# Early products parked in DRAM, value weights split once, gathers tied to single mixing jobs, and four buffers for the sine products

## The chip, the cores and the metric

The kernel runs on one core of one Trainium2 chip. The metric is the device time of one execution in microseconds; the median of the runs counts. PE is the matrix engine, PEld its weight loads, DVE the vector engine, ACT the scalar engine, POOL the GpSimd engine, and SP the engine that issues most loads.

## The reference

One layer of an encoder on 1024 tokens of width 1024, all in fp32. Cut to what matters:

```python
h = _swiglu(_rms_norm(x, g1a), w1_in, w1_out)          # 1024 -> 2 x 2816 -> 1024
x = x + 0.5 * _rms_norm(h, g1b)
m = _token_mixing(_rms_norm(x, gma), w_mix_in, ...)
x = x + _rms_norm(m, gmb)
h = _swiglu(_rms_norm(x, g2a), w2_in, w2_out)
x = x + 0.5 * _rms_norm(h, g2b)

def _token_mixing(u, ...):
    rq, rk, rv, rg, nq, nk, nv, g_ret, g_na = split(u @ w_in)
    q, k = rotary(rq), rotary(rk) * 128**-0.5            # 4 heads of 128
    y = bidirectional retention(q, k, rv)                # 4 heads of 256
    y_ret = (silu(rg) * headnorm(y)) @ w_ret_out
    y_na = neighbourhood_attention(nq, nk, nv) @ w_na_out   # 8 heads of 64, on a 16 x 64 token grid
    return (sigmoid(g_ret) * y_ret + sigmoid(g_na) * y_na) @ w_out
```

## The kernel before

**Precision.** Each fp32 operand is split into a high part (a cast on ACT, line 62) and a low part (a subtraction on DVE, line 63); three matmuls, lines 94 to 96, then make one product of 128 x 128 by 128 x 512: high times high, low times high, high times low. A split weight half is called a piece. Its parts are the tiles `wh` and `wl`, eight buffers each; the raw weights lie in `wraw`, four buffers of 128 x 1024.

**Pairs.** The wide projections run as Strassen-Winograd products on two weight blocks at a time. One such job (`Pairs.run`) makes seven products of 12 matmuls each with the factors `a11`, `s2`, `a12`, `s3`, `s1`, `a22`, `s4` of the activations, and DVE forms the sums of weights (lines 552, 553, 565, 571 or 582) and adds the results (556 to 587). The first feed-forward layer is 22 jobs, the mixing stage 14.

**The start.** `first_factors` normalizes x, transposes its first half, and forms the factors. `a11` and `a12` come from the first half of the tokens and are there first; `s2`, `s3`, `s1`, `a22` and `s4` need the second half and much of DVE. Meanwhile `Pairs.lead` gives PE the two products of a job that need `a11` and `a12` alone, 24 matmuls a job: for jobs 3, 4 and 5 (results copied to SBUF), 0, 1 and 2 (left in PSUM), and 6 (in the two other PSUM banks). A job begun in this way has 60 matmuls left of 84. Between these leads the steps of `first_factors` are written into the program.

**The mixing stage.** Jobs 0 to 3 are queries and keys of the neighbourhood attention, 4, 6, 8 and 10 those of the retention, which `rotate` turns by cosine and sine; 5, 7, 9 and 11 are its gates, 12 and 13 others. Jobs 3, 12 and 13 have been begun earlier and their early products lie in DRAM (`far`, loaded at lines 548 and 549). `rotate` multiplies by the sine into a tile `t` (line 1089), by the cosine in place (1090), stores this, and then has `t` added to the store by two DMAs from POOL (1094, 1095). `t` comes from the same ring of six buffers (`ev`) as the four results of a job. A rotary job also splits the first half of the next job's weights ahead. After job 3 the values of the second half of the tokens are projected (`vproj`), and four DRAM-to-DRAM copies on SP (`nvg<-nv`, line 1443) gather them by column block for the neighbourhood attention.

**The values of the retention.** During the neighbourhood attention (`na_cores`) PE gets other matmuls as filler: first `vproj` for the two column halves of `wrv`. It goes over the tokens in three groups and for each group loads four blocks of weights and splits eight pieces, so 24 loads and 48 pieces in all.

**Order.** A scheduler sets a fixed order of instructions on each engine from dependencies, priorities and its own estimates; `c.after` adds an order between two instructions for it, without a wait on the chip. On ACT, DVE and POOL, and in the queue of SP, an instruction that waits holds up those behind it.

Of the kernel before, what the change touches and what calls it, by code (L numbers as in the profile page):

```python
# [11 lines left out]
F32 = mybir.dt.float32  # L12
# [7 lines left out]
P = 128  # L20
D = 1024
S = 1024
KT = D // P
# [5 lines left out]
NHP = 4  # L29
# [6 lines left out]
KEY_OFF = (0, 8, 24, 32)  # L36
# [399 lines left out]
class Pairs:  # L436
# [49 lines left out]
                    self.begun[i][j] = far[i][j]  # L486
        self.far = far

    def lead(self, save=None, between=(), on_pool=(), abreast=1, extra=0, early=False):

        def split(i):
            if i not in self.fetched:
                self.fetch(i)
            w = self.fetched[i]
            self.ready[i] = self.c.piece(w[:, :512])
            self.fetched[i] = [None, self.c.piece(w[:, 512:])]

        n = self.held + self.saved
        tiles = [i for i in (*range(self.held, n), *range(self.held), *range(n, n + extra)) if i not in self.begun]
        while tiles:  # L500
            group, tiles, abreast = tiles[:abreast], tiles[abreast:], 1
            for i in group:
                if i not in self.fetched:
                    self.fetch(i)
            g = [self.fetched.pop(i) for i in group]
            eng = self.c.nc.gpsimd if group[0] in on_pool else None
            tag = ("ps", 6) if group[0] < n else ("pt", 2)
            ps = [self.products("a11", [self.ready.pop(i) if i in self.ready else w[:, :512] for i, w in zip(group, g)],
                                eng, tag),
                  self.products("a12", [w[1] if isinstance(w, list) else w[:, 512:] for w in g], eng, tag)]  # L510
            if early and tiles:
                split(tiles[0])
            if between:
                f = between.pop(0)()
                if f is not None:
                    between.append(f)
            for i, *pair in zip(group, *ps):
                if self.held <= i < n:
                    sb = [save(), save()]
                    for a, b in zip(sb, pair):  # L520
                        self.c.nc.scalar.copy(a, b)
                    pair = sb
                    self.kept.add(i)
                self.begun[i] = pair

    def behind(self, e):
# [729 lines left out]
def trunk_layer(ctx: ExitStack, tc, x, xt, g1a, w1i, w1o, g1b, gma, wmt, wnv, wrv, logits, dtab, rope, bias,  # L1256
                wro, wno, wmo, gmb, g2a, w2i, w2o, g2b, out):
    nc = tc.nc
# [5 lines left out]
    c = Core(tc, const, wpool, psum, dram)  # L1264
# [3 lines left out]
    def dt(name, shape):  # L1268
        return dram.tile(shape, F32, name=name)
# [8 lines left out]
        "dec": dt("dec", [P, 536]), "far": dt("far", [3, 2, P, 512]), "sr": dt("sr", [8, P, S]), "sn": dt("sn", [8, P, S]), "z": dt("z", [8, P, S]), "m": dt("m", [8, 2, P, S]),  # L1278
    }

    def rows(a):
# [12 lines left out]
    with tc.tile_pool(name="fin1", bufs=1, reuse_waits="tile") as fp:  # L1294
        def lead():
            return early.tile([P, 512], F32, tag="lead", name="lead", bufs=6)

        def sums():
            return early.tile([P, 4, P], F32, tag="cmb", name="cmb", bufs=4).rearrange("p k t -> p (k t)")

        halves = [[sums() for _ in range(2)] for _ in range(2)] + [[lead() for _ in range(2)] for _ in range(2)]
        fin = Pairs(c, wx, [(w1i[i], w1i[FT + i]) for i in LeftFactors.order], 3, 3)
        steps = first_factors(c, wx, fp, g0, halves, sums, lead, pad, x, xt, g1a,
                              lambda j: fin.fetch(3 + j, nc.gpsimd if j < 2 else None))
        next(steps)
        fin.lead(lead, [lambda: next(steps)] * 4, (3, 4), 2, 1)
        for _ in steps:
            pass
        tail = ffn_in(c, fin, fp, LeftFactors(c, early, fp, gl[0]), 40)
# [13 lines left out]
    ahead = {}  # L1323
# [9 lines left out]
    def xh(t, k):  # L1333

        return a21 if (t, k) == (1, 0) else wx.op(("a11", "a12", None, "a22")[2 * t + k])
# [2 lines left out]

    def vproj(src, groups, done):

        for toks in groups:
            banks = {t: c.bank() for t in toks}
            for k in range(KT):
                if k % 2 == 0:
                    w = ahead.pop(k // 2) if k // 2 in ahead else c.load_w(src[k // 2])
                    if k > 3 and qk:
                        c.after(c.fetch, qk)
                        qk.clear()
                for t in toks:
                    tt = slice((t % 4) * P, (t % 4 + 1) * P)  # L1350
                    c.mm3(banks[t], [q[:, k % 4, tt] for q in xh(t // 4, k // 4)], w[k % 2], k == 0, k == KT - 1)
                    yield
            for t in toks:
                done(t, banks[t])
# [43 lines left out]
    with tc.tile_pool(name="pa", bufs=1, reuse_waits="tile") as pa:  # L1398
# [4 lines left out]
        def half():  # L1403
            return pa.tile([P, 512], F32, tag="ev", name="ev", bufs=6)
# [6 lines left out]
        for i, (_, _, f, g, fn) in enumerate(jobs):  # L1411
            parts = {}

            def part(j):
                parts[j] = half()
                return parts[j]

            def done(j):
                h = j % 2
                dst = (f, g)[j // 2][:, h * 512:(h + 1) * 512]  # L1420
                while swaps:
                    swaps.pop()()
                if fn == "rotary":
                    swaps.append(rotate(c, half(), parts[j], *tabs[h], dst, [] if j == 0 else [mx.ahead]))
                    return
                if fn is not None:
                    nc.scalar.activation(parts[j], parts[j], fn)
                c.store(dst, parts[j])
            mx.run(i, part, done, fn == "rotary")
            if i == 2:  # L1430
                x1pool = pool(x1_stack, "x1b", "right")
                a21[:] = [x1pool.tile([P, 4, 512], F32R, name=f"a21{q}") for q in "hl"]
                for k in range(2):
                    raw = c.raw(d["a21"][:, 2 * k:2 * k + 2].rearrange("p k t -> p (k t)"))
# [12 lines left out]
    m_stack, o_stack = ExitStack(), ExitStack()  # L1447
# [237 lines left out]
```

## Time and profile before

| what | before |
|---|---|
| median of three runs | 2220.22 us (2219.85 to 2223.01) |
| profiled execution, its own time | 2219.05 us |
| its span | 2217.2 us |
| granted clock of PE, mean | 0.998 |
| PE busy | 2189.7 us, 99% |
| PEld busy | 1825.6 us, 82% |
| DVE busy | 1589.4 us, 72% |
| ACT busy | 973.8 us, 44% |
| POOL busy | 582.7 us, 26% |
| DMA moved | 448.30 MB |

A busy PE is the union of modelled matmul times, and one matmul of 512 columns is shown with about 390 ns although a new one starts every 0.22 to 0.23 us. So the count of matmuls in a stretch tells more of PE than its busy time does: 90 in 20 us is the most that stretches of 512-column matmuls show. The first feed-forward layer lies at 0 to 652 us, the mixing stage's jobs at about 710 to 985, the neighbourhood attention at 985 to 1152, retention and output projections up to 1525, the second feed-forward layer after that.

### The profile page before, as it was taken

To read this page: it belongs to the slowest core of one execution; us is meant where nothing else is said; L and a number is where in the kernel's file an instruction comes from. 1 tells how busy PE (TensorE), PEld (TensorE's weight loads), DVE (VectorE), ACT (ScalarE), POOL (GpSimd) and SP (SyncE) were. 2 spreads that over 40 slices of the span, in tenths; PEclk is the share of its full clock that TensorE was granted. 3 is DMA by queue.
4 is the path that set the end of the run, shared out by engine and by line. 5 is a ranking of instruction groups with operands and counts; after the bars stand their busy time and mean duration, and the time that the engine had idled before them with its cause. 6 is when DMAs were issued, how large, how long until landed. Compare 5 with 4: busy or idle time off the path is not lost.

```text
span 2217.2 us, 29770 instructions
## 1 busy us (share of the span) xinstructions
PE 2189.7 (99%) x10232; PEld 1825.6 (82%) x10232; DVE 1589.4 (72%) x2796; ACT 973.8 (44%) x1999; POOL 582.7 (26%) x760
## 2 busy tenths in 40 slices
PE   8999999999999999999999999999999999999998
PEld 6788888888888887888888888888888888888887
DVE  8998878665569756779876677553899787867444
ACT  6444434332345322268875565322544343433232
POOL 1121212168422122311101222101112121216942
PEclk9999999999999999999999999999999999999999
DMA  5454434598656564577764466785436343549865
GB/s 218 142 205 148 169 126 179 203 382 298 232 183 200 192 183 133 144 228 237 227 202 144 149 201 225 260 307 190 167 142 221 135 176 133 180 165 372 279 223 185
DMA packets 151734, 448.30 MB, mean 202 GB/s; under 512 B 19488, under 2 KB 46240, under 8 KB 149472
## 3 DMA queue, kind: packets, MB, share of 16 engines
q1 hardware_dynamic: 108592, 308.22, 41.2%
q0 software_dynamic: 42992, 138.20, 17.3%
q8 instruction: 81, 1.33, 0.2%
q14 instruction: 69, 0.57, 0.1%
HBM read 299.78 MB, written 150.75 MB: 203 GB/s over the span
## 4 chain that ended last, share of the span: by engine, by line
PE 89%; DVE 7%; issue 2%; DMA 1%; POOL 1%; ACT 1%; POOLq 0%; SPq 0%; DVEq 0%; ACTq 0%
PE ps L95 27%; PE ps L94 27%; PE ps L96 27%; PE pt L95 1%; PE pt L94 1%; PE pt L96 1%; DVE wl L63 1%; PE ps L962 1%; PE pt L981 1%; POOL rstd L104 0%; PE pt L133 0%; DMA gt<-in_dram 0%; PE pt L1195 0%; DMA vl<-rv 0%; DMA g0s<-gth 0%
## 5 line engine op out<-in xcount | busy, mean ns | idle before, releaser
L63 DVE TENSOR_TENSOR wl<-wraw,wh 128x512 fp32r<-128x512 f32 x472 | 315.1, 688 | 54.6 <-ACT wh L62 54.2
L62 ACT CAST wh<-wraw 128x512 fp32r<-128x512 f32 x476 | 273.5, 618 | 142.8 <-PE ps L95 67.0
L94 PE MATMUL ps<-wh,g 128*128 128x512 f32 x548 | 214.1, 391 | 0.4 <-DVE tmp L231 0.4
L95 PE MATMUL ps<-wl,g 128*128 128x512 f32 x548 | 213.6, 390 | 0.0
L96 PE MATMUL ps<-wh,g 128*128 128x512 f32 x548 | 213.3, 389 | 0.0
L63 DVE TENSOR_TENSOR wl<-w,wh 128x512 fp32r<-128x512 f32 x77 | 79.8, 1057 | 83.1 <-ACT wh L62 82.9
L63 DVE TENSOR_TENSOR wl<-x,wh 128x512 fp32r<-128x512 f32 x77 | 79.5, 1049 | 77.2 <-ACT wh L62 75.6
L62 ACT CAST wh<-t 128x512 fp32r<-128x512 f32 x58 | 36.1, 622 | 210.7 <-DVE t L553 206.7
L94 PEld LDWEIGHTS ps<-wh,g 128*128 128x128 f32 x548 | 102.9, 188 | 21.9 <-DVE tmp L231 0.7
L95 PEld LDWEIGHTS ps<-wl,g 128*128 128x128 f32 x548 | 102.9, 188 | 21.3 <-DVE wl L63 0.5
L96 PEld LDWEIGHTS ps<-wh,g 128*128 128x128 f32 x548 | 102.8, 188 | 21.4
L94 PE MATMUL ps<-a11h,wh 128*128 128x512 f32 x276 | 108.7, 395 | 1.5 <-ACT a11h L62 1.5
L94 PE MATMUL ps<-a22h,wh 128*128 128x512 f32 x280 | 109.9, 393 | 0.0
L95 PE MATMUL ps<-a22l,wh 128*128 128x512 f32 x280 | 109.3, 390 | 0.0
L96 PE MATMUL ps<-a22h,wl 128*128 128x512 f32 x280 | 109.0, 389 | 0.0
L95 PE MATMUL ps<-a11l,wh 128*128 128x512 f32 x276 | 107.9, 391 | 1.0 <-DVE a11l L63 0.8
L94 PE MATMUL ps<-a12h,wh 128*128 128x512 f32 x276 | 108.2, 393 | 0.0
L96 PE MATMUL ps<-a11h,wl 128*128 128x512 f32 x276 | 107.7, 390 | 0.5 <-DVE wl L63 0.5
L96 PE MATMUL ps<-a12h,wl 128*128 128x512 f32 x276 | 107.5, 390 | 0.0
L95 PE MATMUL ps<-a12l,wh 128*128 128x512 f32 x276 | 107.5, 389 | 0.0
L568 DVE TENSOR_TENSOR c<-ps,gt 128x512 f32<-128x512 f32 x44 | 30.4, 691 | 91.5 <-PE ps L96 91.3
L69 POOL DMA_DIRECT2D g0a<-gth x33 | 17.9, 547 | 296.4 <-ACT gth L651 272.3
(439 smaller groups left out, 6316.1 us busy)
## 6 DMA issues: line engine op xcount, KB each, us to landing
wraw<-in_dram SPq DMA_DIRECT2D x203, 512.0 KB, 4.5
g<-g0s SPq DMA_DIRECT2D x44, 512.0 KB, 4.6
g<-g1s SPq DMA_DIRECT2D x44, 512.0 KB, 4.5
g<-g0a SPq DMA_DIRECT2D x33, 512.0 KB, 4.4
g<-g1a SPq DMA_DIRECT2D x33, 512.0 KB, 4.5
g0s<-gth POOLq DMA_DIRECT2D x44, 256.0 KB, 3.9
g0s<-cmb POOLq DMA_DIRECT2D x44, 256.0 KB, 3.8
g1s<-gth POOLq DMA_DIRECT2D x44, 256.0 KB, 3.9
```

The source lines that it names most:

```text
L62: self.done = [nc.scalar.copy(h, src).ins, (eng or nc.vector).tensor_tensor(l, src, hf, ALU.subtract).ins]
L63: (eng or nc.vector).tensor_tensor(l, src, hf, ALU.subtract).ins]
L69: self.nc.gpsimd.dma_start(dst, src)
L94: mm(ps, a[0], b[0], start=start, stop=False, skip_group_check=again)
L95: mm(ps, a[0], b[1], start=False, stop=False, skip_group_check=again)
L96: self.tail = mm(ps, a[1], b[0], start=False, stop=stop, skip_group_check=again).ins.name
L568: self.last = tt(c21, p7, c12, ALU.add).ins
L962: nc.tensor.matmul(bv, q[:, rg * P:(rg + 1) * P], k, start=n == 0, stop=n == 1)
L981: nc.tensor.transpose(pt[:, j * P:(j + 1) * P], s[:, i % 2, (i // 2) * P:(i // 2 + 1) * P], c.ident)
```

## The change

Four edits.

1. `lead` gets jobs 8, 11 and 14 as well, between jobs 5 and 0 of its list. Their two products are copied from PSUM to the tiles `t2` (two buffers) and stored to DRAM (`far1`). In `run` they are loaded back as the far jobs of the mixing stage are. `far2` is allocated and not used.
2. `vproj` keeps the eight pieces of a column half for its three groups of tokens.
3. The four gathers are written one behind each of the mixing jobs 5 to 8, ordered after the job's last addition.
4. The sine products `t` get a ring of four buffers of their own (`evt`).

```diff
-    def lead(self, save=None, between=(), on_pool=(), abreast=1, extra=0, early=False):
+    def lead(self, save=None, between=(), on_pool=(), abreast=1, extra=0, early=False, far={}):
...
         n = self.held + self.saved
-        tiles = [i for i in (*range(self.held, n), *range(self.held), *range(n, n + extra)) if i not in self.begun]
+        self.far = far
+        tiles = [i for i in (*range(self.held, n), *far, *range(self.held), *range(n, n + extra)) if i not in self.begun]
...
-            tag = ("ps", 6) if group[0] < n else ("pt", 2)
+            tag = ("ps", 6) if group[0] < n or group[0] in far else ("pt", 2)
...
+                if i in far:
+                    for a, b in zip(far[i], pair):
+                        e = self.c.wpool.tile([P, 512], F32, tag="t2", name="t2", bufs=2)
+                        self.c.nc.scalar.copy(e, b)
+                        self.c.store(a, e)
+                    pair = far[i]
                 self.begun[i] = pair
...
-        fin.lead(lead, [lambda: next(steps)] * 4, (3, 4), 2, 1)
+        fin.lead(lead, [lambda: next(steps)] * 4, (3, 4), 2, 1,
+                 far={i: d["far1"][n] for n, i in enumerate((8, 11, 14))})
...
     def vproj(src, groups, done):
 
+        w = []
         for toks in groups:
             banks = {t: c.bank() for t in toks}
             for k in range(KT):
-                if k % 2 == 0:
-                    w = ahead.pop(k // 2) if k // 2 in ahead else c.load_w(src[k // 2])
+                if k == len(w):
+                    w += ahead.pop(k // 2) if k // 2 in ahead else c.load_w(src[k // 2])
...
-                    c.mm3(banks[t], [q[:, k % 4, tt] for q in xh(t // 4, k // 4)], w[k % 2], k == 0, k == KT - 1)
+                    c.mm3(banks[t], [q[:, k % 4, tt] for q in xh(t // 4, k // 4)], w[k], k == 0, k == KT - 1)
...
-                    swaps.append(rotate(c, half(), parts[j], *tabs[h], dst, [] if j == 0 else [mx.ahead]))
+                    swaps.append(rotate(c, pa.tile([P, 512], F32, tag="evt", name="evt", bufs=4), parts[j], *tabs[h], dst, [] if j == 0 else [mx.ahead]))
...
-                for cb in range(4):
-                    nc.sync.dma_start(d["nvg"][cb].rearrange("t (r c) d -> (t r) c d", r=4),
-                                      d["nv"][:, KEY_OFF[cb]:KEY_OFF[cb] + 32, :])
+            if NHP < i <= NHP + 4:
+                cb = i - NHP - 1
+                c.after(nc.sync.dma_start(d["nvg"][cb].rearrange("t (r c) d -> (t r) c d", r=4),
+                                          d["nv"][:, KEY_OFF[cb]:KEY_OFF[cb] + 32, :]).ins, [mx.end.name])
```

**DVE at the start.** The last step of the factors `s2` and `s3` and what follows; `wl<-wraw` are the low parts of the leads' pieces, line 420 the sums for `s1`, line 552 the first sum of job 0. Before:

```order
L63 TENSOR_TENSOR s2l<-cmb,s2h 128x512
L63 TENSOR_TENSOR wl<-wraw,wh 128x512 x2
L552 TENSOR_TENSOR wraw<-wraw 128x512
L420 TENSOR_TENSOR g<-g,gt 128x512
L553 TENSOR_TENSOR t_616<-wraw 128x512
```

Now, at the same place:

```order
L63 TENSOR_TENSOR s2l<-cmb,s2h 128x512
L63 TENSOR_TENSOR wl<-wraw,wh 128x512 x6
L420 TENSOR_TENSOR g<-g,gt 128x512
L63 TENSOR_TENSOR wl<-wraw,wh 128x512 x2
L63 TENSOR_TENSOR s1l<-g,s1h 128x512
```

The pieces of jobs 8, 11 and 14 have taken the places of jobs 0, 1 and 2 between the earlier steps, and those of 0, 1, 2 and 6 stand here. From here to the low part of job 0's third product stand 30 instructions before and 34 now.

**DVE in the mixing stage.** The end of job 6 before (`wraw_7320` is the first weight block of job 7, `wraw_7213` the second one of job 6; lines 1089 and 1090 are `rotate`):

```order
L584 TENSOR_TENSOR ev_7296<-ps_7335,ev_7296 128x512
L63 TENSOR_TENSOR wl_7323<-wraw_7320,wh_7322 128x512
L1089 TENSOR_TENSOR ev_7331<-ev_7326,tab_6228 128x512
L1089 TENSOR_TENSOR ev_7351<-ev_7296,tab_6228 128x512
L1090 TENSOR_TENSOR ev_7326<-ev_7326,tab_6227 128x512
L1090 TENSOR_TENSOR ev_7296<-ev_7296,tab_6227 128x512
L63 TENSOR_TENSOR wl_7357<-wraw_7213,wh_7356 128x512
L552 TENSOR_TENSOR wraw_7320<-wraw_7379,wraw_7320 128x512
L553 TENSOR_TENSOR t2_7381<-wraw_7379,wraw_7320 128x512
```

Now the end of job 7 (line 591 was 584 and adds the product with `a22`, line 594 was 587 and adds the last one, with `s4`; `wraw_7557` is the first weight block of job 8):

```order
L584 TENSOR_TENSOR ev_7510<-ps_7493,ev_7491 128x512
L586 TENSOR_TENSOR ev_7429<-ps_7493,ev_7429 128x512
L591 TENSOR_TENSOR ev_7491<-ps_7516,ev_7491 128x512
L594 TENSOR_TENSOR ev_7429<-ps_7536,ev_7429 128x512
L63 TENSOR_TENSOR wl_7564<-wraw_7557,wh_7563 128x512
L559 TENSOR_TENSOR wraw_7557<-wraw_7559,wraw_7557 128x512
L560 TENSOR_TENSOR t2_7561<-wraw_7559,wraw_7557 128x512
```

Before, a low part that job 6 itself still needs (`wl_7357`) stood behind four instructions of `rotate`. Now jobs 4 to 7 have their splits spread between their additions, and job 8's first split stands behind job 7's last addition.

**SP in the mixing stage.** Before, around the gathers (7211 and 7213 are the weights of job 6, 7320 and 7379 those of job 7):

```order
L73 DMA wraw_7211<-in_7_dram 128x1024
L73 DMA wraw_7213<-in_7_dram 128x1024
L1443 DMA nvg_97<-nv_96 16x16384 x4
L73 DMA wraw_7320<-in_7_dram 128x1024
L73 DMA wraw_7379<-in_7_dram 128x1024
```

Now (7352 and 7412 are the weights of job 7, 7557 and 7559 those of job 8, 7872 is one of job 10):

```order
L73 DMA wraw_7352<-in_7_dram 128x1024
L73 DMA wraw_7412<-in_7_dram 128x1024
L1453 DMA nvg_97<-nv_96 16x16384 x3
L73 DMA wraw_7557<-in_7_dram 128x1024
L73 DMA wraw_7559<-in_7_dram 128x1024
...
L73 DMA wraw_7872<-in_7_dram 128x1024
L1453 DMA nvg_97<-nv_96 16x16384
```

The gathers have moved behind two more weight loads, three of them still in a row, and the fourth behind six more.

More of the change, by code (lines that the diff above doesn't have):

```diff
@@ L1277, in trunk_layer @@
         "rv": dt("rv", [TT, P, D]), "rg": dt("rg", [8, P, S]), "ry": dt("ry", [8, P, S]),
-        "dec": dt("dec", [P, 536]), "far": dt("far", [3, 2, P, 512]), "sr": dt("sr", [8, P, S]), "sn": dt("sn", [8, P, S]), "z": dt("z", [8, P, S]), "m": dt("m", [8, 2, P, S]),
+        "dec": dt("dec", [P, 536]), "far": dt("far", [3, 2, P, 512]), "far1": dt("far1", [3, 2, P, 512]), "far2": dt("far2", [3, 2, P, 512]), "sr": dt("sr", [8, P, S]), "sn": dt("sn", [8, P, S]), "z": dt("z", [8, P, S]), "m": dt("m", [8, 2, P, S]),
     }
```

## Prediction

> **What bounds the kernel now.** I read the page's head first, then the stretches of 20 us, then what PE waits for.
>
> ```profile
> span 2217.2 us, 29770 instructions
> PE 2189.7 (99%) x10232; PEld 1825.6 (82%) x10232; DVE 1589.4 (72%) x2796; ACT 973.8 (44%) x1999; POOL 582.7 (26%) x760
> ```
>
> PE is busy for all but 27.5 us, and the change takes no matmul away. So it can only win what PE loses in gaps, and everything hangs on where these lie. The stretches (columns: length, then busy us and instructions of PE, PEld, DVE, ACT, POOL, granted clock, DMA share, GB/s):
>
> ```profile
> 0.00:20.00 20.00, 11.99 (x56) 9.20 (x57) 11.56 (x18) 12.36 (x25) 7.66 (x12) 1.00 0.91 349
> 40.00:60.00 20.00, 19.43 (x86) 15.77 (x85) 19.81 (x34) 10.17 (x16) 0.00 (x0) 1.00 0.24 80
> 60.00:80.00 20.00, 16.95 (x62) 12.96 (x62) 16.23 (x27) 7.56 (x13) 0.75 (x1) 0.83 0.31 95
> 100.00:120.00 20.00, 19.44 (x85) 15.24 (x84) 19.78 (x34) 9.05 (x17) 1.82 (x4) 1.00 0.40 142
> 120.00:140.00 20.00, 19.19 (x84) 15.05 (x83) 18.83 (x32) 8.59 (x16) 7.50 (x14) 1.00 0.63 235
> 720.00:740.00 20.00, 19.23 (x85) 15.63 (x84) 15.75 (x29) 6.50 (x10) 2.70 (x5) 1.00 0.39 136
> 800.00:820.00 20.00, 20.00 (x90) 16.57 (x89) 13.14 (x22) 2.77 (x5) 3.59 (x6) 1.00 0.66 201
> 840.00:860.00 20.00, 17.48 (x76) 13.81 (x76) 15.41 (x25) 3.05 (x6) 7.46 (x10) 1.00 0.47 104
> 940.00:960.00 20.00, 20.00 (x90) 16.57 (x89) 14.96 (x25) 10.62 (x16) 3.52 (x6) 1.00 0.73 200
> 980.00:1000.00 20.00, 19.56 (x100) 16.51 (x99) 15.98 (x44) 16.26 (x38) 2.15 (x3) 1.00 0.59 196
> 1000.00:1020.00 20.00, 19.48 (x117) 16.92 (x117) 18.12 (x52) 15.84 (x45) 2.19 (x3) 1.00 0.88 259
> 2200.00:2220.00 20.00, 9.58 (x43) 7.60 (x41) 10.51 (x15) 2.17 (x6) 5.43 (x6) 0.86 0.28 105
> ```
>
> Full rate is 90 matmuls of 512 columns in 20 us, 0.222 us each (row 800 to 820). Against 90, PE lacks 4 matmuls in 40 to 60, 28 in 60 to 80, 5 and 6 in 100 to 140, 5 in 720 to 740 and 14 in 840 to 860. At 0.222 us that is 0.9, 6.2, 1.1, 1.3, 1.1 and 3.1 us. The first and the last row are the kernel's start and end, which the change does not touch. In the rows at 980 and 1000 forms are mixed, and the idle 0.44 and 0.52 us count. All within reach is thus 9.5 us in the first feed-forward layer, 4.2 in the mixing stage and 1.0 in the attention.
>
> **The long early loss.** In the order of time, with what ended the idle time in brackets:
>
> ```profile
> 60.73 0.39 PE L95 MATMUL ps<-s1l,wh 128*128 128x512 f32 x1
> 63.40 0.69 DVE L63 TENSOR_TENSOR wl<-wraw,wh 128x512 fp32r<-128x512 f32 x1
> 64.14 0.79 PE L96 MATMUL ps<-s1h,wl 128*128 128x512 f32 x1 [3.02 <-DVE wl L63]
> 64.73 0.63 PE L94 MATMUL ps<-s1h,wh 128*128 128x512 f32 x1
> 69.65 0.70 PE L94 MATMUL ps<-s4h,wh 128*128 128x512 f32 x1
> 70.19 0.39 PE L95 MATMUL ps<-s4l,wh 128*128 128x512 f32 x1
> ```
>
> PE stands with job 0's third product until DVE has made that piece's low part, and DVE (19.81 of 20 us busy in the stretch before) was still making factors. The next 13 matmuls, 64.14 to 70.19, take 6.05 us where 13 x 0.222 = 2.9 would do: the granted clock is down (0.83 over the stretch). So a wait of about 3.2 us cost 3.1 more.
>
> **Part 1, early products of jobs 8, 11 and 14.** PE gets 3 x 24 = 72 matmuls, 72 x 0.222 = 16.0 us, ahead of job 0, and has them less in jobs 8, 11 and 14. DVE gets 4 instructions more ahead of the awaited split (34 for 30). Their price and that of ACT's casts:
>
> ```profile
> L63 DVE TENSOR_TENSOR wl<-wraw,wh 128x512 fp32r<-128x512 f32 x472 | 315.1, 688 | 54.6 <-ACT wh L62 54.2
> L62 ACT CAST wh<-wraw 128x512 fp32r<-128x512 f32 x476 | 273.5, 618 | 142.8 <-PE ps L95 67.0
> ```
>
> 315.1 / 472 = 0.67 us, so the split comes 4 x 0.67 = 2.7 us later while PE comes 16.0 later. Of the 3.2 us it lacked, 16.0 - 2.7 - 3.2 = 10.1 us become slack: the stall goes whole, and with it the slow clock (-6.2), and the 0.9 of 40 to 60, where PE waits for a copy on ACT that stands behind a factor:
>
> ```profile
> PE ps L94 <- ACT gt L551: 0.6, 1, 0.6
> ```
>
> On ACT come 6 casts and 6 copies at 0.62, 7.4 us, into stretches where it is idle (9.83 of 20 us at 40 to 60); the leads that PE does first cover them. If that cover fails, the next thing late is the high part of a lead's piece.
>
> The two later losses look alike:
>
> ```profile
> 102.91 0.50 PE L94 MATMUL ps<-s2h,wh 128*128 128x512 f32 x1 [0.56 <-ACT wh L62]
> 131.57 0.50 PE L94 MATMUL ps<-s2h,wh 128*128 128x512 f32 x1 [0.81 <-ACT wh L62]
> ```
>
> They are 28.66 us apart, the time of two begun jobs; 120 matmuls need 26.7. DVE (19.78 busy in the row 100 to 120) sets that pace. Slack won earlier isn't carried on whole, since DVE must wait for PE's results between; but the new order has its splits of jobs 0 and 1 ahead of those results, one or two instructions (0.67 to 1.3 us) in front of where they were, and each of the losses is 1.1 to 1.3. Bounds: none and all of 2.4; I take 1.8, as the first should vanish and the second halve. In jobs 8, 11 and 14 DVE has as much per job as in other begun jobs, but full jobs of 84 matmuls (18.7 us) stand around each, where the loss does not occur: 0.
>
> The parked results cost 6 stores of 256 KB and 6 loads, and three weight blocks are fetched a second time. The mixing stage does the same with its far jobs:
>
> ```profile
> far<-ev POOLq DMA_DIRECT2D x6, 256.0 KB, 5.6
> ev<-far SPq DMA_DIRECT2D x6, 256.0 KB, 4.4
> SPq L548 <- DMA rq<-ev: 6.3, 1, 6.3
> ```
>
> There SP once stood 6.3 us for a buffer with weight loads queued behind it, and PE still ran at 90 (row 940 to 960). I take 0. The added addition per far job (c11 is loaded, not read from PSUM) is 0.67 us on DVE, hidden by the longer neighbours.
>
> **Part 2, kept value splits.** 16 loads, 32 casts and 32 subtractions go: 19.8 us of ACT and 21.4 of DVE, all beside PE work. In that stage PE waits for splits twice, and only the second lies in the second group of tokens:
>
> ```profile
> 1008.11 0.50 PE L95 MATMUL ps<-wl,a11h 128*128 128x512 f32 x1 [0.52 <-DVE wl L63]
> ```
>
> -0.5. All eight buffers stay held until the third group; the second half's first piece then has the rest of that group to be made, 7 x 6 matmuls, 9.3 us, against 1.3 for cast and subtraction, so no wait.
>
> **Parts 3 and 4, gathers and sine buffers.** The gathers landed in 10.1 us and PE was full (row 800 to 820); DVE lost 4.1 us waiting for a sine buffer, in the same full row. By themselves both are worth 0:
>
> ```profile
> nvg<-nv SPq DMA_DIRECT2D x4, 10.1
> 813.90 0.69 DVE L1089 TENSOR_TENSOR ev<-ev,tab 128x512 f32<-128x512 f32 x1 [1.36 <-DMA rq<-ev]
> 818.52 0.69 DVE L1089 TENSOR_TENSOR ev<-ev,tab 128x512 f32<-128x512 f32 x1 [2.72 <-DMA rq<-ev]
> ```
>
> What counts is the order of DVE that comes with them. The loss at 840 to 860:
>
> ```profile
> 847.99 0.39 PE L96 MATMUL ps<-a22h,wl 128*128 128x512 f32 x1
> 848.41 0.69 DVE L584 TENSOR_TENSOR ev<-ps,ev 128x512 f32<-128x512 f32 x1 [1.43 <-PE ps L96]
> 849.02 0.68 DVE L63 TENSOR_TENSOR wl<-wraw,wh 128x512 fp32r<-128x512 f32 x1
> 849.62 1.29 DVE L1089 TENSOR_TENSOR ev<-ev,tab 128x512 f32<-128x512 f32 x2
> 849.76 0.50 PE L96 MATMUL ps<-a11h,wl 128*128 128x512 f32 x1 [0.48 <-DVE wl L63]
> 852.02 0.69 DVE L63 TENSOR_TENSOR wl<-wraw,wh 128x512 fp32r<-128x512 f32 x1
> 852.77 0.51 PE L96 MATMUL ps<-s4h,wl 128*128 128x512 f32 x1 [2.04 <-DVE wl L63]
> ```
>
> DVE makes the low part behind four rotary instructions while PE stands. In the new order this place is regular: -3.1. But job 8's first split now stands behind job 7's last addition. The rows price that: from the start of the product's last matmul (847.99) to the first matmul with the new low part (849.76) are 1.77 us, and three matmuls cover 0.67: +1.1. The clock stays, as it did after 2.04 us here. Net -2.0; bounds -3.1 and, if the old loss comes back whole in job 8, 0. The wait at 720 to 740 has the same order before and now: 0.
>
> **The sum.** -6.2 - 0.9 - 1.8 - 0.5 - 2.0 = -11.4 us. The profiled execution took 2219.05 (its span and 1.85 around it) and so becomes 2207.7; the median of the runs shown, 2220.22, stands 1.2 higher, so I forecast 2208.8.
>
> **The clock, by rows and by a page.** The rows say: 3.2 us of waiting was followed by half rate for 6.05. The Trainium skill, "TensorE: Matmul & The Clock Gate", Part 1, says that PE falls to half its clock after an idle window of about 3.4 us, a window that runs freely, and is let up again after about 3.4 us of work. Half the rate agrees; here less waiting sufficed and the half rate lasted longer. By the page the slow stretch would be worth 1.7 us and not 3.1, and the sum -10.0; I go by the rows.
>
> **Rivals.**
> - *DVE keeps the pace.* The two later losses stay (+1.8) and job 8 gets the whole old loss (+2.0): -7.6, about 2212.6. For it: DVE is 95 to 99% busy there. Against it: in the new order the splits stand earlier.
> - *The early part gives little.* If `t2`'s two buffers hold up ACT until stores land, a lead's cast behind them comes late, and PE stands among the leads instead. A lead takes 24 x 0.222 = 5.3 us and a store 5.6 in the far row above, so 0.3 per lead is likely at worst, 1 us in all; only if POOL's stores took twice as long would 3 x 5.3 = 16 be lost against 8.9. A third of that, 5 us, gives 2213.8, and with no change in the mixing stage 2215.8: within 0.2% of no change (4.4 us, about what a measurement of this kernel can tell).
> - *SP blocks the far jobs; slower.* The load of a far result waits for a buffer of job 5, 8 or 11 whose stores are on POOL, and the weights of the job after it queue behind. If SP stood longer there than the weights are ahead, about one job or 18.7 us, PE would stand in three jobs. With 3.2 + 3.1 us each (wait and slow clock, as at 64) that is 18.9 - 11.4 = +7.5, 2227.7; it decides from 3 us of waiting per job on. Against it stands the 6.3 us row above without loss.
> - *The gathers aren't one per job.* The order shows three in a row still, so that edit does not do what it says; its effect is in the order of DVE alone, and is in the sum.
>
> **How the numbers follow.** As forecast within 3 us: 0.62. DVE keeps the pace: 0.24. Little from the early part: 0.10, of which most stays within 0.2% or just past it. Blocked far jobs or another new wait: 0.04. The low end has all losses gone: 9.5 + 3.1 + 0.5 = 13.1, 2207.1, less a microsecond for the spread of runs: 2206. The high end takes in the first rival and part of the second: 2214. Faster by over 0.2% 0.88, within 0.2% 0.08, slower 0.04.
>
> **What would show it.** Right: no row under 88 matmuls between 40 and 140 us and a granted clock of 1.00 there; PE at 90 in the stretch where it now has 76, and one wait for `wl` of about 1 us some 20 us later, at job 8's start; one wait for `wl` fewer in the attention; about 32 fewer casts and subtractions. Wrong: a clock below 1.00 anywhere past 20 us, PE waits for casts among the leads, or for far results at jobs 8, 11 and 14.

## The result and the profile after

| | before | after |
|---|---|---|
| median of 21 runs each | 2220.22 us (2218.36 to 2223.56) | 2217.51 us (2215.02 to 2220.59) |
| profiled execution | 2219.05 us | 2220.59 us |

The ratio is 0.9984, 95% interval 0.9978 to 0.9991: 2.7 us faster by the medians and 2.0 to 4.9 us by the interval, where 11.4 were forecast and 2206 to 2214 was the range. The execution that was profiled after the change is the slowest of its 21, so its trace is read for places and for what waits; what an edit is worth is taken from the comparisons. Its head:

```profile
span 2218.8 us, 29691 instructions
PE 2192.1 (99%) x10232; PEld 1828.2 (82%) x10232; DVE 1572.3 (71%) x2767; ACT 960.7 (43%) x1970; POOL 588.3 (27%) x766
```

DVE has 29 instructions less, ACT 29 less. The stretches that answer to those of before (length, then busy us and instructions of PE, PEld, DVE, ACT, POOL, granted clock, DMA share, GB/s):

```profile
60.00:80.00 20.00, 20.00 (x90) 16.33 (x88) 15.91 (x27) 10.56 (x18) 0.00 (x0) 1.00 0.15 52
100.00:120.00 20.00, 19.79 (x86) 15.57 (x85) 19.20 (x33) 8.69 (x15) 7.51 (x14) 1.00 0.63 237
120.00:140.00 20.00, 19.71 (x87) 15.98 (x86) 18.28 (x31) 7.58 (x14) 6.45 (x12) 1.00 0.62 224
140.00:160.00 20.00, 18.82 (x81) 15.08 (x82) 19.79 (x34) 10.98 (x20) 2.35 (x5) 1.00 0.42 144
700.00:720.00 20.00, 16.57 (x71) 13.41 (x70) 9.36 (x27) 4.86 (x8) 1.10 (x2) 0.95 0.42 139
720.00:740.00 20.00, 20.00 (x79) 16.30 (x78) 18.55 (x47) 6.31 (x12) 2.28 (x5) 0.87 0.40 132
840.00:860.00 20.00, 20.00 (x90) 16.54 (x89) 15.48 (x25) 4.55 (x8) 9.18 (x12) 1.00 0.52 124
860.00:880.00 20.00, 18.00 (x72) 14.14 (x71) 11.50 (x18) 6.84 (x12) 2.26 (x4) 0.91 0.33 96
1000.00:1020.00 20.00, 20.00 (x118) 17.49 (x119) 14.52 (x48) 13.82 (x40) 1.10 (x2) 1.00 0.63 178
```

Three of them before:

```profile
140.00:160.00 20.00, 20.00 (x90) 16.57 (x89) 19.06 (x33) 8.46 (x15) 6.40 (x12) 1.00 0.70 247
700.00:720.00 20.00, 20.00 (x90) 16.53 (x89) 18.56 (x58) 9.76 (x19) 1.82 (x3) 1.00 0.56 199
860.00:880.00 20.00, 20.00 (x90) 16.57 (x89) 13.63 (x22) 8.16 (x15) 3.94 (x6) 1.00 0.62 185
```

The long early loss is gone (62 matmuls before, 90 now, clock 1.00), and so is the one at 840 to 860. Three new ones stand in their place: 9 matmuls at 140 to 160, 19 and 11 at 700 to 740, 18 at 860 to 880, the last two with a lower clock. A matmul that reaches over the edge of a row is counted in both rows, so the balance is taken from counts that run from the kernel's start: PE is 31 matmuls ahead of before at 80 us, 36 at 140, 30 at 200 and at 700, 5 at 740, 19 at 860 and 1 at 880. At full rate one starts every 0.227 us (857.71 to 860.66 in the trace after: 13 of them), so 30 are 6.8 us. The early gain is there, and nearly all of it is lost again at 700 to 740 and at 860 to 880.

**At 719: a load of 4 KB behind weights.** From the timeline after, by engine: SP's queue, DVE, PE (numbers: start, duration; in brackets the idle time ahead and what ended it):

```profile
691.29 14.29 SPq L73 DMA_DIRECT2D wraw<-in_dram  x3
705.63 2.08 SPq L1418 DMA_DIRECT2D tab<-in_dram  x4
707.75 0.91 SPq L1057 DMA_DIRECT2D decx<-in_dram  x1
...
716.64 0.18 DVE L1060 TENSOR_SCALAR dect<-decx 128x8 f32<-128x8 f32 x1 [9.67 <-DMA decx<-in_dram]
718.26 0.69 DVE L571 TENSOR_TENSOR ev<-ps,ev 128x512 f32<-128x512 f32 x1
...
719.00 0.79 PE L94 MATMUL ps<-s1h,wh 128*128 128x512 f32 x1 [3.43 <-DVE ev L571]
725.10 0.40 PE L96 MATMUL ps<-a22h,wl 128*128 128x512 f32 x1
```

The same load and its first use before:

```profile
701.08 0.48 SPq L1050 DMA_DIRECT2D decx<-in_dram  x1
...
712.21 0.19 DVE L1053 TENSOR_SCALAR dect<-decx 128x8 f32<-128x8 f32 x1
...
722.23 0.68 DVE L564 TENSOR_TENSOR ev<-ps,ev 128x512 f32<-128x512 f32 x1
```

After job 3's products DVE computes the decays of the retention from the small table `decx`. Before, SP issued that load 11.1 us ahead of its use. Now a pair of weight loads, which wait for their buffers, stands ahead of the tables in SP's queue: the program comes to this place 6.6 us earlier (the transposes ahead of the mixing stage begin at 622.4 us instead of 629.0), `decx` is issued 6.7 us later, and it lands 8.9 us after its issue instead of 5.8. DVE stands 9.67 us, line 571 behind it, and PE behind line 571. DVE's order has changed too: the addition of line 571 (564 before) stood behind the whole computation of the decays, whose last instruction starts at 721.88, and now stands behind the first eight instructions that follow from `decx`. From 719.00 to 725.10 there are 14 matmuls, 0.44 us each.

**At 871: a cast behind four activations.** The timeline after, at the start of job 8:

```profile
869.02 0.69 DVE L594 TENSOR_TENSOR ev<-ps,ev 128x512 f32<-128x512 f32 x1 [2.03 <-PE ps L96]
...
869.79 0.63 ACT L1436 ACTIVATE ev<-ev 128x512 f32<-128x512 f32 x1 [2.13 <-DVE ev L594]
870.33 0.60 ACT L62 CAST wh<-wraw 128x512 fp32r<-128x512 f32 x1
...
870.98 0.50 PE L94 MATMUL ps<-a11h,wh 128*128 128x512 f32 x1 [2.00 <-ACT wh L62]
875.23 0.39 PE L95 MATMUL ps<-a11l,wh 128*128 128x512 f32 x1
```

ACT makes the high part of job 8's first piece only after the last silu of job 7, which waits for job 7's last addition. The two loads of its raw weights were issued at 855.1 and 855.7 and landed within 4.7 to 6.1 us, so these are not what is late. Ten matmuls then take 4.25 us, 0.43 each.

**At 141: a buffer that is still being stored.** The factors of the first layer are split into `gth` (high part, four buffers) and stored from POOL:

```profile
134.98 0.62 ACT L658 CAST gth<-cmb 128x512 fp32r<-128x512 f32 x1 [4.26 <-DMA g0a<-gth]
135.63 0.69 DVE L659 TENSOR_TENSOR cmb<-cmb,gth 128x512 fp32r<-128x512 f32 x1 [0.63 <-ACT gth L658]
137.33 0.69 DVE L659 TENSOR_TENSOR cmb<-cmb,gth 128x512 fp32r<-128x512 f32 x1 [1.01 <-ACT gth L658]
137.94 0.69 DVE L559 TENSOR_TENSOR wraw<-wraw 128x512 f32<-128x512 f32 x1
141.19 0.50 PE L94 MATMUL ps<-s2h,wh 128*128 128x512 f32 x1 [1.47 <-ACT wh L62]
```

A cast waits for a store to land, DVE waits for the cast, and the sums of the next job's weights (line 559) stand behind. DVE was busy for most of the stretch, but it was also waiting, twice.

### The profile page after: what moved, and what is told of

Same layout as the page of the kernel before. It is cut to its first block, busy times and chain, and to the rows that moved or that the text cites. A ratio compares the mean times of both kernels' runs of the same rounds, so it can differ in the third digit from the quotient of the medians.

```text
span 2218.8 us, 29691 instructions
## 1 busy us (share of the span) xinstructions
PE 2192.1 (99%) x10232; PEld 1828.2 (82%) x10232; DVE 1572.3 (71%) x2767; ACT 960.7 (43%) x1970; POOL 588.3 (27%) x766
## 4 chain that ended last, share of the span: by engine, by line
PE 90%; DVE 3%; issue 2%; DMA 2%; ACT 2%; POOL 1%; SPq 0%; POOLq 0%; DVEq 0%; ACTq 0%
PE ps L95 28%; PE ps L94 28%; PE ps L96 28%; PE pt L95 1%; PE pt L96 1%; PE pt L94 1%; PE pt L988 1%; PE ps L969 1%; DMA g0s<-gth 1%; PE pt L133 0%; POOL rstd L104 0%; DMA vl<-rv 0%; DMA decx<-in_dram 0%; DVE wl L63 0%; ACT wh L62 0%
## 5 line engine op out<-in xcount | busy, mean ns | idle before, releaser
L63 DVE TENSOR_TENSOR wl<-wraw,wh 128x512 fp32r<-128x512 f32 x440 | 292.7, 686 | 59.1 <-ACT wh L62 58.4
L62 ACT CAST wh<-wraw 128x512 fp32r<-128x512 f32 x444 | 255.9, 618 | 149.8 <-PE ps L95 65.7
L94 PE MATMUL ps<-s1h,wh 128*128 128x512 f32 x232 | 91.5, 394 | 3.4 <-DVE ev L571 3.4
L62 ACT CAST wh<-w 128x512 fp32r<-128x512 f32 x77 | 46.6, 620 | 110.9 <-PE pt L96 54.5
```

The lines of the kernel that those rows point to most:

```text
L62: self.done = [nc.scalar.copy(h, src).ins, (eng or nc.vector).tensor_tensor(l, src, hf, ALU.subtract).ins]
L63: (eng or nc.vector).tensor_tensor(l, src, hf, ALU.subtract).ins]
L94: mm(ps, a[0], b[0], start=start, stop=False, skip_group_check=again)
```

## The experiments

Each of the first three losses got a kernel that takes its supposed cause away from the changed kernel, or undoes the edit. All ratios are to the kernel before. After that come the edits one at a time, and the versions with several causes removed. A difference to the changed kernel, in us, is one of medians that were taken at different times. By the ratios and their intervals it is 4.4 us, give or take 3.1, without edit 4, and 2.0, give or take 2.5, for the fifth buffer; so the smaller differences rest on the rows, and the time alone does not show them.

### Without edit 4

```diff
-swaps.append(rotate(c, pa.tile([P, 512], F32, tag="evt", name="evt", bufs=4), parts[j], ...
+swaps.append(rotate(c, half(), parts[j], ...
```

> The changed kernel without edit 4: the sine products come from the ring of six again; the other three edits stay. The changed kernel lost 26 matmuls (30 for 4 before) at 700 to 740, where PE stood 3.43 us for line 571 on DVE, and DVE had stood 9.67 us for the load decx of the decays; SP had issued that load behind a pair of weight loads that waited for their buffers. Theory A: edit 4 alone moves the table and decay loads behind that pair. Then the stall goes and this kernel takes 2217.5 - 5.6 = about 2212 us, with decx issued some 20 us before DVE needs it and a clock of 1.00 at 700 to 740. Rival B: the early products of edit 1 bring the mixing stage to this place 7 us earlier and the loads are late whatever their order: then the stall stays, about 2217.5. The loss of 18 matmuls at 860 to 880 stays by both.

Measured: 2212.06 us, ratio 0.9964 (0.9952 to 0.9977). From its timeline (SP) and then its stretches:

```profile
693.75 0.48 SPq L1057 DMA_DIRECT2D decx<-in_dram  x1
```

```profile
700.00:720.00 20.00, 19.22 (x85) 15.61 (x84) 17.80 (x60) 7.07 (x14) 1.24 (x3) 1.00 0.25 86
720.00:740.00 20.00, 20.00 (x90) 16.57 (x89) 16.80 (x27) 6.57 (x11) 4.18 (x8) 1.00 0.57 198
860.00:880.00 20.00, 18.00 (x78) 14.11 (x77) 14.99 (x24) 7.52 (x14) 1.63 (x3) 1.00 0.40 145
```

`decx` is issued 14.0 us earlier than with edit 4 and the stall is gone: PE waits 0.78 us for line 571, as it did before, and the time is that of theory A. `decx` is issued 11.2 us ahead of its use, not the 20 that were expected. The clock stays 1.00 at job 8's start too, so not all of the difference to the changed kernel need come from 719. Four more buffers in a pool, meant for DVE's rotary work 100 us later, moved other loads in SP's queue. Why the scheduler does that was not followed further.

### The decays' loads on another queue

```diff
-nc.sync.dma_start(x, logits)
+nc.gpsimd.dma_start(x, logits)
```

(and so for `dectb` and `decd`).

> The changed kernel, with the three small loads of the decays (decx, dectb, decd) issued from POOL instead of SP; nothing else. Theory A: PE's stall at 719 is DVE waiting for decx, which queues on SP behind weight loads. On another queue it lands early, DVE's order there becomes that of the kernel before, with its loss of 1.1 us: 2217.5 - 5.6 + 0.0 = about 2212 (1.1 us of loss stood there before and is in the 5.6 already), clock 1.00. Rival B: the stall is DVE's own work (the decay chain itself stands ahead of line 571 whatever its loads do): then about 2217.

Measured: 2212.03 us, ratio 0.9962 (0.9949 to 0.9976). The load on POOL's queue, and the stretch at 700 (the next one has 90 matmuls):

```profile
696.00 0.61 POOL L1057 DMA_DIRECT2D decx<-in_dram  x1
```

```profile
700.00:720.00 20.00, 20.00 (x88) 16.07 (x87) 16.84 (x58) 6.49 (x14) 2.18 (x4) 1.00 0.47 152
```

Edit 4 is still there, with the same weight loads ahead of the tables on SP, and the stall is not: `decx` is used at 706.54 without a wait. DVE's order is another here as well, with line 571 behind most of the decays, and PE does not wait for it. So the sine buffers cost nothing by themselves: their price is the late `decx`.

### A fifth buffer for the high parts

```diff
-tag="gth", name="gth", bufs=4
+tag="gth", name="gth", bufs=5
```

> The changed kernel with five buffers instead of four for gth, the high parts of the factors that the first layer stores; the order of instructions on DVE is unchanged. In the changed kernel DVE stands 0.46 us at 108, 0.63 and 1.01 at 135 to 137, and 0.22 and 1.04 at 164 to 166 for casts on ACT that wait for a gth whose store has not landed, and PE then lacks 16 matmuls (3.6 us) between 100 and 160. Theory A: this chain of cast, store and cast sets the pace there, not DVE: with a fifth buffer one of the two waits per pair of jobs goes whole and the other shrinks, 1.5 to 3.6 us gained: 2214 to 2216. Rival B: DVE is simply full: no change, 2217.5.

Measured: 2214.47 us, ratio 0.9975 (0.9966 to 0.9984).

```profile
100.00:120.00 20.00, 20.00 (x88) 16.09 (x87) 19.66 (x34) 8.70 (x15) 7.52 (x14) 1.00 0.65 238
120.00:140.00 20.00, 20.00 (x89) 16.26 (x88) 19.91 (x34) 9.84 (x18) 6.49 (x12) 1.00 0.69 258
140.00:160.00 20.00, 20.00 (x88) 16.37 (x88) 19.80 (x33) 9.37 (x17) 3.95 (x8) 1.00 0.43 150
```

By the rows PE lacks 5 matmuls here instead of 16, and by 200 us it has done 848 from the kernel's start instead of 838: 2.3 us, and the rest of the 3.0 lies within the interval. DVE has no wait for a cast left in this stretch, and is busier with the same instructions. The store chain set the pace in the changed kernel, not DVE: theory A. The kernel before was not run with a fifth buffer.

### Without edit 3, and edit 3 alone

The gathers behind job 3 again, with the rest of the change:

> The changed kernel without edit 3: the four gathers stand in a row behind job 3 again; the other three edits stay. Theory A: the place of the gathers sets both the loss that went (14 matmuls, 3.1 us, at the end of job 6, where four rotary instructions stood ahead of a split) and the one that came (18 matmuls, 4.0 us, at the start of job 8, where the cast of its first piece stands on ACT behind job 7's four activations). Then the first comes back and the second goes: 2217.5 + 3.1 - 4.0 = about 2216.6, and the loss at 700 to 740 stays. Rival B: the loss at job 8 comes from the other sine buffers or from the early products: then it stays, and with the old one back the time is 2217.5 + 3.1 = about 2220.6.

Measured: 2217.23 us, ratio 0.9989 (0.9980 to 0.9998).

Edit 3 on the kernel before:

> The kernel before with edit 3 alone (the gathers written behind jobs 5 to 8). Theory A: the loss of 14 matmuls at the end of job 6 goes (-3.1) and job 8's start loses 2.0 us of waiting, and 0.7 to 2.0 us more with the matmuls at half rate, if the clock drops: before - 0.4 to + 0.9, so 2219.6 to 2220.9, no difference. Rival B: job 8's loss needs the other edits: then before - 3.1, 2216.9.

Measured: 2220.36 us, ratio 0.9996 (0.9987 to 1.0005). The two stretches, first without edit 3, then with it alone:

```profile
840.00:860.00 20.00, 17.48 (x77) 13.82 (x76) 16.10 (x26) 4.44 (x8) 7.29 (x10) 1.00 0.57 121
860.00:880.00 20.00, 20.00 (x90) 16.57 (x89) 12.25 (x20) 6.77 (x12) 3.94 (x6) 1.00 0.53 169
```

```profile
840.00:860.00 20.00, 20.00 (x90) 16.56 (x89) 16.35 (x26) 4.11 (x8) 8.40 (x12) 1.00 0.49 117
860.00:880.00 20.00, 18.00 (x71) 14.13 (x70) 10.57 (x17) 7.27 (x13) 3.02 (x5) 0.91 0.34 94
```

In both pairs of kernels, which differ in edit 3 alone, the loss moves with the gathers: edit 3 takes it from the end of job 6 to the start of job 8. The times agree with theory A both ways, and by time alone neither could be told from no difference to its own base.

### The early products, the sine buffers and the value splits, each alone

> The kernel before with edit 1 alone (early products of jobs 8, 11 and 14). In the changed kernel PE was 36 matmuls ahead at 140 us and, after the loss at the next job, 26 ahead at 200, 5.8 us, and no loss came in jobs 8, 11 and 14. Theory A: that is all of edit 1, and nothing of it is given back later: before - 5.8 = about 2214.2, with the loss at 840 to 860 (14 matmuls) as before and full rate at 700 to 740 but for the 1.1 us of before. Rival B: the mixing stage loses at 720 because the early part came forward by 6 us: then before - 5.8 + 5.6 - 1.1, about 2219.

Measured: 2214.69 us, ratio 0.9971 (0.9961 to 0.9982), 6.1 us gained. PE is 27 matmuls ahead of before at 200 us and at 700, counted from the kernel's start, and 27 are 6.1 us. (In the changed kernel it is 30 by this count; the 26 of the expectation are summed from rows.) Nothing is given back at 720 (86 and 90 matmuls in the two stretches, where before has 90 and 85), so rival B falls. One row is worse than before: 840 to 860 has 64 matmuls at a clock of 0.83, where before has 76 at 1.00. The wait is the same (2.04 us), the clock is not; more of this below.

> The kernel before with edit 4 alone (four buffers of their own for the sine products). Its SP order has the table and decay loads behind one more pair of weight loads. Theory A: this costs here what it cost in the changed kernel, a stall of 2.4 to 3.4 us at line 571 (564 before) and the slow clock after it, less the 1.1 us that stood there before: before + 3 to 5.6 = 2223 to 2226; the waits of DVE for a sine buffer (4.1 us) go and give PE nothing. Rival B: in the kernel before DVE comes to the place later against its loads, so the loads are there and the time stays at 2220.

Measured: 2223.55 us, ratio 1.0011 (1.0003 to 1.0020). DVE waits 8.35 us for `decx`, PE 2.10 us for line 564. By the medians edit 4 costs 2.7 us alone and 5.5 within the change. Alone, PE's wait is shorter (2.10 us for 3.43) and the clock stays at 1.00 after it.

> The kernel before with edit 2 alone (value splits kept). By the sum of the prediction: the wait of 0.52 us at 1008 goes, 2220.5 - 0.5 = 2220.0. Rival: PE in the attention waits elsewhere for the same DVE and ACT, which have 41 us less to do but not at that place: no change, 2220.5; or, with DVE and ACT freer in all, up to 2 us gained, 2218.5.

Measured: 2219.05 us, ratio 0.9994 (0.9985 to 1.0003). The wait of 0.52 us at 1008 is gone, as it is in the changed kernel; whether the whole is faster by that, the runs don't tell.

### Job 8's piece made ahead, with two causes removed

Without edit 4, with five `gth` buffers, and:

```diff
-mx.run(i, part, done, fn == "rotary")
+mx.run(i, part, done, 4 <= i < 11)
```

> The changed kernel without edit 4, with five gth buffers, and with the first piece of the next job split ahead in the gate jobs of the mixing stage too (it was so in the rotary jobs alone), so that the casts of jobs 8 and 10 no longer stand behind four activations. If the three losses are independent, their gains add: 2217.5 - 5.6 (stall at 719, edit 4) - 3.0 (gth, as measured) - 2.7 to 4.0 (job 8's start) = 2205 to 2206. Rival: DVE takes the earlier splits of job 8 from job 7's additions and PE waits for these instead: then 2209.

Measured: 2216.23 us, ratio 0.9978 (0.9969 to 0.9987). A miss by 10 us. From its timeline:

```profile
859.01 0.63 ACT L1436 ACTIVATE ev<-ev 128x512 f32<-128x512 f32 x1 [2.09 <-DVE ev L591]
859.54 1.12 ACT L62 CAST wh<-wraw 128x512 fp32r<-128x512 f32 x2
860.72 0.50 PE L94 MATMUL ps<-s4h,wh 128*128 128x512 f32 x1 [2.47 <-ACT wh L62]
```

With job 8's piece ahead, job 7's own last cast came to stand behind job 7's activations, and job 9's likewise at 903.54, again 2.47 us. The cure made the same fault one piece earlier, twice, each followed by a lower clock (0.91 over 860 to 880 and over 900 to 920).

### Gathers later, and gathers that stand alone

Behind jobs 10 to 13, with the rest of the change:

> The changed kernel with the gathers behind jobs 10 to 13 instead of 5 to 8; nothing else. In its order job 6 keeps the split between its rotary instructions (as in the changed kernel), and the casts of job 8's first piece stand ahead of job 7's last activations on ACT (as in the kernel before). Theory A: then both the loss at the end of job 6 and the one at the start of job 8 are gone, full rate from 740 to 980: 2217.5 - 2.7 (the wait of 2.0 and its edges at full clock) to 4.0 (with the half rate that the changed kernel showed) = 2213.5 to 2214.8. Rival B: the gathers, now next to the first loads of the attention, come late for it, and PE waits past 985 instead: 2217 or more.

Measured: 2218.26 us, ratio 0.9993 (0.9984 to 1.0002). Theory A falls, and rival B has the time but not the cause. From 760 to 940 PE runs at the full rate, and the loss appears at job 12, before the attention:

```profile
956.38 0.63 ACT L1436 ACTIVATE ev<-ev 128x512 f32<-128x512 f32 x1 [2.09 <-DVE ev L594]
957.75 0.62 ACT L62 CAST wh<-t 128x512 fp32r<-128x512 f32 x1 [0.75 <-DVE t L560]
958.43 0.80 PE L94 MATMUL ps<-s2h,wh 128*128 128x512 f32 x1 [2.81 <-ACT wh L62]
```

The fault is of the same kind as at job 8, with one difference. The cast that PE waits for stands behind job 11's last activation here too, but what it waits for itself is DVE's sum of weights (line 560), which stands behind job 11's last addition (line 594, at 955.65). The four gathers are not three in a row here: SP issues two at 907.0 and two at 946.8.

The same with two causes removed, and with the decays' loads from POOL besides:

> The changed kernel without edit 4, with five gth buffers, and with the gathers behind jobs 10 to 13. If the three losses are independent, their gains add: 2217.5 - 5.5 (edit 4, as measured) - 3.0 (gth, as measured) - 2.7 to 4.0 (late gathers, by the rows) = 2205.0 to 2206.3. Rival: as with the version that split job 8 ahead, a new place in the mixing stage waits instead; then 2209 or more.

> As the version with three losses removed (no edit 4, five gth buffers, gathers behind jobs 10 to 13), and the decays' three loads from POOL besides. With the decays' loads from POOL the wait of 0.75 us at line 571 near 715 was gone in the changed kernel's variant, and 88 and 90 matmuls stood in the two stretches where 85 and 90 stand without: 0.7 us less than the three together, 2204.3 to 2205.6. Rival: no difference between the two.

Measured: 2212.91 us, ratio 0.9963 (0.9951 to 0.9976), and 2213.36, ratio 0.9967 (0.9954 to 0.9979). Both miss their forecast by 7 to 8 us, as the rivals had it: they lose 21 and 23 matmuls at 940 to 960, behind the same wait of 2.81 us, and the loads from POOL added nothing here.

One gather behind each gate job, with the rest of the change:

```diff
-if NHP < i <= NHP + 4:
-    cb = i - NHP - 1
+if i in (5, 7, 9, 11):
+    cb = (i - 5) // 2
```

> The changed kernel with one gather behind each of the gate jobs 5, 7, 9 and 11 instead of 5 to 8; nothing else. Three in a row put one job's casts behind four activations of the job before it, at job 8 (wait of 2.00 us) and, with the gathers later, at job 12 (2.81 us). In this kernel's order the four gathers stand alone, each behind a pair of weights, job 6's split keeps its place between the rotary instructions, and no job's first cast stands behind four activations. Theory A: several gathers in a row ahead of weights are what makes that order; then neither loss appears, full rate from 740 to 980, and the stall at 719 stays: 2217.5 - 2.7 to 4.0 = 2213.5 to 2214.8. Rival B: the gathers themselves, running beside the weights, delay them wherever they are, and some job waits for its raw weights: 2217 or more.

Measured: 2212.48 us, ratio 0.9965 (0.9951 to 0.9978): 5.0 us less than the changed kernel, a little more than theory A had. The former loss at job 8, and 940 to 960, where the later gathers lost 18:

```profile
860.00:880.00 20.00, 20.00 (x90) 16.57 (x89) 13.57 (x23) 6.12 (x11) 2.52 (x5) 1.00 0.52 159
940.00:960.00 20.00, 20.00 (x90) 16.58 (x89) 16.29 (x28) 13.19 (x20) 3.28 (x6) 1.00 0.67 224
```

So gathers need not cost anything: rival B falls. Four in a row went with a loss at the end of job 6, three in a row with one at job 8, two and two with one at job 12, and four that stand alone with none. That points to theory A, but the place of the gathers changed along with their grouping, and why the scheduler's order of ACT and DVE follows them was not traced. (The expectation takes the later gathers for three in a row; they stood two and two.) All three causes removed:

> The changed kernel without edit 4, with five gth buffers, and with the gathers behind the gate jobs 5, 7, 9 and 11. If the three losses are independent: 2217.5 - 5.5 (edit 4, as measured) - 3.0 (gth, as measured) - 2.7 to 4.0 (job 8's start, by the rows) = 2205.0 to 2206.3, and no stretch of 20 us between 740 and 980 under 88 matmuls. Rival: a wait appears at another job, as at job 12 with the later gathers: 2209 or more.

Measured: 2206.76 us (2205.77 to 2206.90), ratio 0.9938 (0.9925 to 0.9950). This beats both kernels, by 13.1 us the one before and by 10.8 the changed one, and it lies 0.5 us above the range that was expected. Every stretch of 20 us from 740 to 960 has 90 matmuls; two earlier ones that had lost:

```profile
140.00:160.00 20.00, 20.00 (x89) 16.34 (x88) 19.80 (x34) 9.40 (x17) 3.90 (x8) 1.00 0.41 145
720.00:740.00 20.00, 20.00 (x90) 16.55 (x89) 16.29 (x25) 5.39 (x8) 3.77 (x7) 1.00 0.60 198
```

## Why the prediction was wrong

By its steps, the forecast beside what the count of matmuls from the kernel's start gives (0.227 us each, both profiled executions):

| step | forecast, us | counted, us |
|---|---|---|
| early stall and its slow clock, 40 to 80 | -7.1 | -7.0 (31 matmuls) |
| the two later losses, 100 to 180 | -1.8 | +0.2 (1 matmul; the losses moved to 141 and did not shrink) |
| value splits | -0.5 | -0.5 (wait gone) |
| 700 to 740 | 0 | +5.7 (25 matmuls) |
| end of job 6 and start of job 8 | -2.0 | +0.9 (14 lacking before, 18 now) |

The counted steps sum to -0.7, and the start of the same instruction in both traces agrees: the first transpose of the retention's results (`yn`) starts at 1201.2 before and at 1200.7 now. The profiled execution is 1.5 us longer all the same, since it loses 2.2 us in the retention from there on, a stage that the prediction does not treat: the first product of the projection behind it (with `xy`) starts at 1398.0 before and at 1399.7 now. In the sixteen traces this stretch takes 196.5 to 199.0 us, most in the changed kernel, and its cause stays open. The median of the changed kernel lies 3.1 us below the execution that was profiled; which of the losses were smaller in the others, no trace shows.

- **The early stall was right.** Its mechanism, its place and its size hold: 7.0 us by 80 us, and edit 1 alone gains 6.1. PE waits for no cast among the leads, and for no far result (DVE waits for one twice, 2.3 us in all, and PE is busy meanwhile); the rivals "the early part gives little" and "SP blocks the far jobs" fall.
- **"The wait at 720 to 740 has the same order before and now: 0" is the step that failed most: +5.7 us.** The order is not the same: line 571 on DVE stood behind all of the decays and now stands near their start. And what the decays wait for comes from SP, whose order at this place is not in the prediction: `decx` is late there, and PE waits 3.43 us behind it. The same goes for "By themselves both are worth 0": undone, edit 4 gives 5.5 us back by the medians. No rival names this mechanism; "another new wait" has a share of 0.04. The signs of a wrong forecast did name a clock below 1.00, and it came: 0.95, 0.87, 0.91.
- **"DVE sets that pace" failed.** Being busy 19.78 of 20 us was taken as being the bound. DVE was waiting for casts even before, just ahead of the two losses:

```profile
99.05 0.69 DVE L652 TENSOR_TENSOR cmb<-cmb,gth 128x512 fp32r<-128x512 f32 x1 [0.81 <-ACT gth L651]
127.71 0.69 DVE L652 TENSOR_TENSOR cmb<-cmb,gth 128x512 fp32r<-128x512 f32 x1 [1.06 <-ACT gth L651]
```

  The rival "DVE keeps the pace" was right that these losses stay and that job 8 gets a whole loss, but its time (2212.6) was not, and its reason was wrong: a fifth store buffer, which takes nothing from DVE, brought 2.3 us there.
- **"+1.1" for job 8 was the right place and the wrong engine.** The price was taken from a wait for DVE's low part. PE waited for ACT's high part, which stood behind four activations; ACT's order was not read. The wait was 2.00 us, and "the clock stays, as it did after 2.04 us here" did not hold: of the 4.0 us lost, about 2.0 are the half rate.
- **"The gathers aren't one per job"** was right in that three stood in a row. That its effect is in DVE's order alone was wrong: on ACT it cost what it gained on DVE. With each gather behind a gate job of its own, neither loss is there.

The first three edits as they are gave 2212.06 us. With the gathers spread, and without the fifth buffer, they would give 2206.8 and the buffer's 3.0, about 2209.8, an estimate. So the forecast's 2208.8 is close to what these edits are worth where job 8's start does not wait.

## What to carry to other kernels

Where a scheduler sets the order of all engines, compare the order on every engine and in every load queue at the places where PE has little slack, not on the busiest engine alone: here four extra buffers in one pool delayed a 4 KB load in a queue, and with copies moved in that queue, casts came to stand behind activations on another engine. A busy share near 100% does not show that an engine is the bound; look for its waits in the same stretch first. And when a cure moves a loss instead of removing it, as with the later gathers and with the pieces split ahead, the cause has not been reached yet.

## What the runs showed of the hardware

The half clock does not follow from the length of a wait alone. The same wait, at the same place of the program, in profiled executions of several kernels (matmuls in the stretch of 20 us around it, at most 90):

| wait of PE | clock stayed 1.00 | clock fell |
|---|---|---|
| 2.00 us, start of job 8 | 78 and 78 (no edit 4; five buffers) | 72, 72, 71 at 0.91 (changed kernel; decays from POOL; edit 3 alone) |
| 2.04 us, end of job 6 | 76, 77, 76 (before; no edit 3; edit 2 alone) | 64 at 0.83 (edit 1 alone), 69 at 0.91 (edit 4 alone) |
| 3.02 us, at 64 | none | 62 at 0.83 (before), 65, 66 and 66 at 0.91 (edits 4, 3 and 2 alone) |

Counting 0.222 us for each of the matmuls that such a row lacks, one wait of about 2 us costs from 2.7 to 5.8 us. Two more waits of this length, 1.98 us at 716 (gathers behind jobs 10 to 13) and 2.10 us at 724 (edit 4 alone), left the clock at 1.00. All 13 waits of 2.45 us or more past the first 20 us of the sixteen traces were followed by a lower clock. The stall at 719 cost 30 matmuls after 3.43 us of waiting in the changed kernel, and 20 after 2.70 us in the one with five buffers. The Trainium skill, "TensorE: Matmul & The Clock Gate", Part 1, has the clock halved after an idle window of about 3.4 us that runs freely and does not start with the work. That it runs freely fits that equal waits end differently; but here about 2.0 us of waiting were enough in 5 of 12 cases, well under the page's figure, so its length cannot be read as a safe limit. That the phase of such a window decides was not tested by itself.
